# The first filter of a two-layer diffusion trunk, moved from ahead of the first norm to beside it

## The chip, the cores and the metric

The kernel runs on one core of a Trainium2 chip, as one launch. The metric is the device time of that launch in microseconds (us). TensorE does the matmuls, VectorE (DVE) and ScalarE (ACT) the elementwise work and the evacuation of psum, GpSimd (POOL) a few loads, and SyncE (SP) issues nearly all DMA. Each engine works through its own list in order and waits on semaphores for the others.

## The reference, cut to what matters

Two streams, 128 prompt tokens and 1024 sample tokens of width 1024, pass two layers. The sample stream gets a grid position embedding first. Each layer normalises, projects once into four groups of mixers (GLA, a gated linear recurrence with a short convolution, Hyena, HGRN2), joins them, and then runs a gated feed-forward.

```python
xs = x_sample + grid_position_embedding(...)          # 1024 x 1024
mod = silu(c) @ w_mod[l] + b_mod[l]                   # six vectors a layer
u = rmsnorm(x, norm1_g) * (1 + sc1) + sh1
proj = u @ w_in                                       # all mixers' inputs
...
def hyena_filters(L, ...):                            # needs no token at all
    h = sin(sin(pe @ w1 + b1) @ w2 + b2) @ w3
    h = h * exp(-dist * decay_rate)
    return h / sum(abs(h))
full = irfft(rfft(z, n=2L) * rfft(h, n=2L))           # long convolution
```

Four Hyena filters are needed: two layers, each for the sample (L = 1024) and the prompt (L = 128). Each is made in two steps: its taps (h, its weighting by the decay and the sum of its absolute values) and its spectra (sums and differences of halves, then matmuls with transform matrices). None depends on the tokens.

## The kernel before

Tokens lie along the free dimension: 1152 columns, prompt and sample together, cut into three blocks of 384, and the 1024 channels lie in eight tiles of 128 partitions. Two channel tiles of x share a buffer of 128x2304 f32 (1152 KB), so x is four loads; a piece of the modulation weights is 128x2048 f32 (1024 KB). Line 298 is the helper through which all matmuls go, so its rows are told apart by tiles: `pm<-u,ws` are projections (`u` the normalised tokens, `ws` split weights), `pm<-ws,u` the value projections, `ps<-fX,fw` filter taps, `ps<-fH,fM` spectra with the transform matrices `fM`, `ps<-rgx,rgw` the recurrent gates, `pa<-wm,cT` the modulation. One f32 row of a matmul in program order is recorded as two in the trace.

The work that the change touches, in the names of the profile of before:

- `x_in` loads x, adds the position embedding (L1825, VectorE), squares it (L1828 and L1831, ScalarE), sums the squares over the eight channel tiles (L1832, VectorE), sums over partitions on TensorE with ones (`pa`), makes the mean (`hss`, L1841) and an inverse root by some sixteen small VectorE operations (L496 to L508, `rp`).
- `norm_u` transposes and broadcasts that root on TensorE, and makes `ut` (L569) and `u` (L572) on VectorE.
- `taps` of a filter loads its weights and decay into `fX`, and does nine rounds for the sample (five for the prompt): a matmul into `ps`, an exponential `fwn` (L1146, ScalarE), a product `fH` (L1147, VectorE), an absolute value `fab` (L1153, ScalarE), a running sum in `fX` (L1154, VectorE). Then two sums on TensorE (`ones`).
- `spectra` makes sums and differences of the taps (L1189 to L1198), matmuls with `fM`, and stores (L1220, L1222). `fil_mats` (L1232) loads `fM`, four pieces of 576 KB.
- `hgrn_items` are projections whose psum (two buffers, tag m) ScalarE reads twice, into `TT` and `KK` with a sigmoid (L853). `v_proj` evacuates by plain copies (L816). `rg_core` runs the gates: sigmoids (L1032), tanh (L1040), exponential (L1044), square (L1045), square root (L1050) on ScalarE, products and scans on VectorE (L1046 to L1066). Functions that don't share a table cost ScalarE an ACT_TABLE_LOAD between them.

The program is written as generators. `turns` takes a step of each of its generators in rotation. `weave` and `run_norm` run a main generator, and after each step take items from a fill queue (projections) for as many nanoseconds of TensorE as that step declares, so the written order mixes both. A scheduler then orders each engine's list. `filters_b` returns the two generators of one filter, here t0 and s0 for layer 0 of the sample, t1 and s1 for layer 1, tp0, sp0, tp1, sp1 for the prompt.

Of the kernel before, what the change touches and what calls it, by code (L numbers as in the profile page):

```python
# [26 lines left out]
DEPTH = 2  # L27
# [250 lines left out]
class Trunk:  # L278
# [7 lines left out]
    NM = (4, 6)  # L286
# [129 lines left out]
    def mod_load(s, l, c, i):  # L416

        w = s.d("wm")[:, :2048]
        s.nc.sync.dma_start(w.rearrange("p (j n) -> p j n", j=4), s.A["w_mod"][l, c, i])
        if l == 0 and c == s.NM[0] - 1 and i == 1:  # L420
            s.behind = s.nc.cur_bb.bb.instructions[-1]
        return w
# [691 lines left out]
    def taps(s, l, which, box, V):  # L1114
# [8 lines left out]
        X = s.d("fX")  # L1123
        hx = X[:2, 1024:1536]
# [6 lines left out]
        if which == "s":  # L1131
            MV = s.fil_mats()
        else:
            MV = [X[:P, 2048 + 48 * i:2096 + 48 * i].unsqueeze(1) for i in range(5)]
            for i in range(5):
                nc.sync.dma_start(MV[i], s.A["fil_p"][i] if i < 4 else s.A["fin_p"])

# [36 lines left out]
        nc.vector.tensor_tensor(out=ht(0)[:1], in0=ht(0)[:1], in1=sk, op=ALU.add)  # L1174
        V.X, V.ht, V.hx, V.MV = X, ht, hx, MV
        yield

    def spectra(s, l, which, box, V):
# [3 lines left out]
        X, ht, hx, MV = V.X, V.ht, V.hx, V.MV  # L1182
# [620 lines left out]
    def x_in(s, box, V):  # L1803
# [3 lines left out]
        for i in range(4):  # L1807
# [8 lines left out]

        pieces = ((0, 512, s.fw[:, 0:512]), (512, 768, V.H[0][:, 2048:2304]), (768, 1024, V.H[1][:, 2048:2304]),
                  (1024, 1152, s.fw[:, 512:640]))
# [16 lines left out]
        ssq = s.p("a")  # L1835
        for (a, b, ac) in pieces:
            for c in range(a, b, 128):
                i = c // 128
# [6 lines left out]
    def main(s):  # L1845
# [5 lines left out]
        with tc.tile_pool(name="dp", bufs=19) as dp, tc.tile_pool(name="gp", bufs=1) as gp, \  # L1851
# [66 lines left out]
            fb = {w: [] for w in "sp"}  # L1918
# [5 lines left out]
            box = []  # L1924
            (t0, s0, V0), (t1, s1, _) = [s.filters_b(l, "s", fb["s"]) for l in range(DEPTH)]
            (tp0, sp0, _), (tp1, sp1, _) = [s.filters_b(l, "p", fb["p"]) for l in range(DEPTH)]
            ch = itertools.chain
            xi = s.x_in(box, V0)
            na, nb = s.NM
            for _ in s.turns([ch(t0, itertools.islice(s0, nb)), xi, s.mods_pe(0, 0, na, s.AH)]):  # L1930
                pass
            x, xt, y = box

            def rest():
                for _ in s0:
                    yield 2700
            s.fill_add([s.item(rest)], None)
# [4 lines left out]
            def late():  # L1942
                yield from s.mods_pe(0, na, 12, 2)
                s.fill_add([s.v_proj(0, 1, st.u, st.vh)], ("vh", 0))
            s.weave(s.turns([ch(t1, s1, tp0, sp0, tp1, sp1), late()]), s.WB)
# [17 lines left out]
```

## Time and profile before

| | us |
| --- | --- |
| median of 3 runs | 3343.38 (3341.73 to 3345.31) |
| profiled execution, its own time | 3340.47 |
| its span in the trace | 3338.4 |
| first projection matmul starts | 91.24 |
| first gate matmul starts | 272.97 |
| mean granted clock of TensorE | 0.991 of full speed |

The rows further down come from the one profiled execution. A row of a timeline is a run of like instructions on one engine: start, length, engine, line, operation, output and inputs, shape, count, and in brackets how long the engine had stood idle just before and which instruction released it. A row of windows gives the busy time of each engine inside a stretch. The clock column is the granted TensorE clock as a share of 2.4 GHz.

### The profile page before, as it was taken

To read this page: it belongs to the slowest core of one execution; us is meant where nothing else is said; L and a number is where in the kernel's file an instruction comes from. 1 tells how busy PE (TensorE), PEld (TensorE's weight loads), DVE (VectorE), ACT (ScalarE), POOL (GpSimd) and SP (SyncE) were. 2 spreads that over 40 slices of the span, in tenths; PEclk is the share of its full clock that TensorE was granted. 3 is DMA by queue.
4 is the path that set the end of the run, shared out by engine and by line. 5 is a ranking of instruction groups with operands and counts; after the bars stand their busy time and mean duration, and the time that the engine had idled before them with its cause. 6 is when DMAs were issued, how large, how long until landed. Compare 5 with 4: busy or idle time off the path is not lost.

```text
span 3338.4 us, 55402 instructions
## 1 busy us (share of the span) xinstructions
PE 3250.3 (97%) x23886; PEld 3029.7 (91%) x23886; DVE 1742.9 (52%) x3412; ACT 1008.9 (30%) x1774; POOL 27.6 (1%) x101
## 2 busy tenths in 40 slices
PE   7999999999999999999999999999999999999998
PEld 3657878899999999999998888889999999999997
DVE  6635885648463444444457787665653322232326
ACT  5437354333231111111125535432332111111112
POOL 0000000000000000000000000000000000000000
PEclk8999999999999999999999999999999999999999
DMA  7541101224121121222212110113310111111112
GB/s 278 176 158 32 50 17 34 69 103 150 39 80 64 69 91 58 86 73 73 73 58 92 36 45 22 43 60 127 133 51 26 45 45 40 46 36 45 46 45 75
DMA packets 72992, 241.10 MB, mean 72 GB/s; under 512 B 14319, under 2 KB 26469, under 8 KB 60972
## 3 DMA queue, kind: packets, MB, share of 16 engines
q1 hardware_dynamic: 70844, 223.22, 19.2%
q0 software_dynamic: 1904, 14.35, 1.2%
q8 instruction: 187, 3.06, 0.4%
q14 instruction: 57, 0.47, 0.0%
HBM read 207.99 MB, written 29.56 MB: 71 GB/s over the span
## 4 chain that ended last, share of the span: by engine, by line
PE 84%; DVE 9%; ACT 5%; issue 1%; DMA 1%; SPq 0%; DVEq 0%; ACTq 0%
PE pm L298 54%; PE ps L298 26%; PE pa L298 3%; PE pa L301 1%; DVE QQ L686 1%; DVE KK L682 1%; DVE DS L685 1%; DVE ws L342 1%; DVE rgri L1060 0%; ACT ws L341 0%; DMA wr<-w 0%; DVE TT L687 0%; ACT rgri L1032 0%; DVE rgab L1055 0%; ACT rgab L1044 0%
## 5 line engine op out<-in xcount | busy, mean ns | idle before, releaser
L298 PE MATMUL pm<-u,ws 128*128 128x384 f32 x9792 | 1793.0, 340 | 13.5 <-ACT KK L853 4.0
L298 PEld LDWEIGHTS pm<-u,ws 128*128 128x128 f32 x9792 | 1703.1, 188 | 44.6 <-issue 9.5
L298 PE MATMUL ps<-hid,ws 128*128 128x384 f32 x3168 | 559.0, 337 | 0.0
L298 PEld LDWEIGHTS ps<-hid,ws 128*128 128x128 f32 x3168 | 553.7, 188 | 0.6 <-DVE hid L1766 0.2
L341 ACT CAST ws<-wr 128x1024 fp32r<-128x1024 f32 (+3 forms) x234 | 220.3, 941 | 659.5 <-PE ps L298 396.2
L342 DVE TENSOR_TENSOR ws<-wr,ws 128x1024 fp32r<-128x1024 f32 (+3 forms) x234 | 254.6, 1088 | 215.3 <-ACT ws L341 214.3
L1764 DVE TENSOR_TENSOR sg<-sg,pm 128x384 f32<-128x384 f32 x132 | 73.0, 553 | 463.5 <-PE pm L298 463.4
L1508 DVE SCALAR_TENSOR_TENSOR x<-ps,mod,x 128x256 f32<-128x256 f32 (+1 forms) x320 | 158.2, 515 | 275.7 <-PE ps L298 274.4
L1765 ACT CAST hid<-sg 128x384 fp32r<-128x384 f32 x132 | 67.7, 513 | 474.1 <-DVE sg L1764 474.0
L298 PE MATMUL pm<-mh,ws 128*128 128x384 f32 x1152 | 203.8, 337 | 0.7 <-DVE x L1508 0.7
L298 PEld LDWEIGHTS pm<-mh,ws 128*128 128x128 f32 x1152 | 200.9, 188 | 1.6 <-DVE x L1508 1.4
L1758 ACT ACTIVATE sg<-pm 128x384 f32<-128x384 f32 x132 | 64.6, 489 | 225.1 <-PE pm L298 225.1
L470 DVE SCALAR_TENSOR_TENSOR acc<-wm,cT,acc 128x512 f32<-128x512 f32 x168 | 116.1, 745 | 0.2 <-DMA wm<-w_mod 0.2
L298 PEld LDWEIGHTS pm<-ws,u 128*128 128x128 f32 x864 | 107.7, 188 | 8.7 <-issue 3.8
L298 PE MATMUL pm<-ws,u 128*128 128x272 f32 (+1 forms) x864 | 114.9, 289 | 0.6 <-DVE lr L818 0.4
L1766 DVE TENSOR_TENSOR hid<-sg,hid 128x384 fp32r<-128x384 f32 x132 | 73.6, 558 | 58.2 <-ACT hid L1765 58.2
L298 PEld LDWEIGHTS ps<-QQ,DS 64*64 64x64 f32 x3456 | 67.9, 134 | 36.2 <-issue 14.8
L682 DVE TENSOR_TENSOR KK<-KK,TT 128x640 f32<-128x640 f32 x112 | 92.3, 824 | 9.9 <-PE pa L301 6.8
L685 DVE COPY_PREDICATED DS<-masks,ps 128x320 f32<-128x320 uint8 x192 | 89.2, 478 | 14.4 <-PE ps L298 13.7
L298 PE MATMUL ps<-QQ,DS 64*64 64x64 f32 x3456 | 86.0, 230 | 9.3 <-DVE QQ L686 3.5
L686 DVE TENSOR_TENSOR QQ<-QQ,TT 128x640 f32<-128x640 f32 x112 | 91.7, 819 | 2.3 <-PE ps L298 1.8
L541 ACT ACTIVATE sq<-x 128x384 f32<-128x384 f32 x84 | 43.8, 523 | 142.1 <-DVE x L1508 109.0
(307 smaller groups left out, 2623.1 us busy)
## 6 DMA issues: line engine op xcount, KB each, us to landing
wm<-w_mod SPq DMA_DIRECT2D x48, 1024.0 KB, 6.5
wr<-w SPq DMA_DIRECT2D x96, 512.0 KB, 3.3
wr<-w_in SPq DMA_DIRECT2D x48, 512.0 KB, 3.5
dft<-dft_s POOLq DMA_DIRECT2D x12, 1152.0 KB, 5.4
wr<-w SPq DMA_DIRECT2D x32, 320.0 KB, 2.9
xscr<-x SPq DMA_DIRECT2D x8, 1152.0 KB
x<-xscr SPq DMA_DIRECT2D x8, 1152.0 KB, 5.3
wr<-w_out SPq DMA_DIRECT2D x16, 512.0 KB, 3.2
```

The costliest lines, as they stand in the source:

```text
L298: return s.nc.tensor.matmul(out, lhsT, rhs, start=start, stop=stop)
L341: nc.scalar.copy(w[:, 0, :n], raw[:, :n])
L342: nc.vector.tensor_tensor(out=w[:, 1, :n], in0=raw[:, :n], in1=w[:, 0, :n].bitcast(F32), op=ALU.subtract)
L470: nc.vector.scalar_tensor_tensor(out=acc[:, x], in0=wk, scalar=cc, in1=acc[:, x], op0=ALU.mult, op1=ALU.add)
L682: nc.vector.tensor_tensor(out=ka, in0=ka, in1=cap(TT, o + T + h, [[2 * h, n], [-(T + h), 2], [0, h]]), op=ALU.mult)
L685: nc.vector.copy_predicated(Dt[g][:, j], s.masks[:, li].unsqueeze(1).to_broadcast([128, nb, 64]), ps[j])
L686: nc.vector.tensor_tensor(out=qa, in0=qa, in1=cap(TT, o + h, [[2 * h, n], [T - h, 2], [0, h]]), op=ALU.mult)
L1508: nc.vector.scalar_tensor_tensor(out=x[k][:, a:b], in0=ps[:, a - g * GS:b - g * GS], scalar=gcol[:, k, st:st + 1], in1=x[k][:, a:b], op0=A ...
L1758: nc.scalar.activation(out=sg, in_=ps, func=AF.Silu)
L1764: nc.vector.tensor_tensor(out=sg, in0=sg, in1=pp[1], op=ALU.mult)
L1765: nc.scalar.copy(hi[:, 0, sl], sg)
L1766: nc.vector.tensor_tensor(out=hi[:, 1, sl], in0=sg, in1=hi[:, 0, sl].bitcast(F32), op=ALU.subtract)
```

## The change

The first filter's taps and half of its spectra ran in turns with the loading of x, its squares and the first modulation vectors; the rest of its spectra were a fill item beside the first norm. Now x and the modulation vectors come alone; the taps of the first filter are the fill item beside the first norm (behind the recurrent mixer's projections), and its spectra stand at the head of the chain of the other filters, which are woven with the fill queue. The transform matrices are loaded when the first spectra begin. The running sums of squares, which lay in gaps of three tiles in four pieces, get a tile `ssq` and three pieces. The fill queue and all other code stay.

```diff
--- before.py
+++ after.py
@@ -283,7 +283,7 @@
     ORD = ((0, 1, 2), (2, 1, 0))
 
     LG = ((0, 5), (5, 9))
-    NM = (4, 6)
+    NM = 4
     WB = 1800
     AH = 3
     VP, VB = (2, 3, 3), ((1, 2), (0,))
@@ -417,7 +417,7 @@
 
         w = s.d("wm")[:, :2048]
         s.nc.sync.dma_start(w.rearrange("p (j n) -> p j n", j=4), s.A["w_mod"][l, c, i])
-        if l == 0 and c == s.NM[0] - 1 and i == 1:
+        if l == 0 and c == s.NM - 1 and i == 1:
             s.behind = s.nc.cur_bb.bb.instructions[-1]
         return w
 
@@ -1128,9 +1128,8 @@
         sk = X[:1, 1536:2048] if l else s.fh[:1, 1800:2312] if which == "s" else None
         if sk is not None:
             nc.sync.dma_start(sk, s.A["hy_skip"][l])
-        if which == "s":
-            MV = s.fil_mats()
-        else:
+        MV = None
+        if which == "p":
             MV = [X[:P, 2048 + 48 * i:2096 + 48 * i].unsqueeze(1) for i in range(5)]
             for i in range(5):
                 nc.sync.dma_start(MV[i], s.A["fil_p"][i] if i < 4 else s.A["fin_p"])
@@ -1179,7 +1178,7 @@
         nc = s.nc
         h = HC[which]
         Q, P, NT, ncol = h["Q"], h["P"], h["NT"], h["ncol"]
-        X, ht, hx, MV = V.X, V.ht, V.hx, V.MV
+        X, ht, hx, MV = V.X, V.ht, V.hx, V.MV or s.fil_mats()
         if which == "s":
             iP, iM, iRp, iRm = 0, 3, 6, 7
         else:
@@ -1800,7 +1799,7 @@
                 else:
                     yield w
 
-    def x_in(s, box, V):
+    def x_in(s, box):
 
         nc, A = s.nc, s.A
         x, xt = s.xtiles()
@@ -1813,9 +1812,8 @@
         nc.sync.dma_start(pr, A["pos_row"])
         nc.sync.dma_start(pc, A["pos_col"])
         yield
-
-        pieces = ((0, 512, s.fw[:, 0:512]), (512, 768, V.H[0][:, 2048:2304]), (768, 1024, V.H[1][:, 2048:2304]),
-                  (1024, 1152, s.fw[:, 512:640]))
+        sq = s.d("ssq")
+        pieces = [(a, b, sq[:, a:b]) for a, b in ((0, 512), (512, 1024), (1024, 1152))]
         for k in range(KT):
             xs = x[k][:, :L_S].rearrange("p (a b) -> p a b", b=64)
             if k < 4:
@@ -1922,19 +1920,18 @@
             for _ in s.turns([s.filters_a(w, fb[w]) for w in "sp"]):
                 pass
             box = []
-            (t0, s0, V0), (t1, s1, _) = [s.filters_b(l, "s", fb["s"]) for l in range(DEPTH)]
+            (t0, s0, _), (t1, s1, _) = [s.filters_b(l, "s", fb["s"]) for l in range(DEPTH)]
             (tp0, sp0, _), (tp1, sp1, _) = [s.filters_b(l, "p", fb["p"]) for l in range(DEPTH)]
             ch = itertools.chain
-            xi = s.x_in(box, V0)
-            na, nb = s.NM
-            for _ in s.turns([ch(t0, itertools.islice(s0, nb)), xi, s.mods_pe(0, 0, na, s.AH)]):
+            na = s.NM
+            for _ in s.turns([s.x_in(box), s.mods_pe(0, 0, na, s.AH)]):
                 pass
             x, xt, y = box
 
-            def rest():
-                for _ in s0:
+            def taps():
+                for _ in t0:
                     yield 2700
-            s.fill_add([s.item(rest)], None)
+            s.fill_add([s.item(taps)], None)
             st, gen = s.open(0, x, y, None)
             s.run_norm(gen)
             s.x_out(0, xt)
@@ -1942,7 +1939,7 @@
             def late():
                 yield from s.mods_pe(0, na, 12, 2)
                 s.fill_add([s.v_proj(0, 1, st.u, st.vh)], ("vh", 0))
-            s.weave(s.turns([ch(t1, s1, tp0, sp0, tp1, sp1), late()]), s.WB)
+            s.weave(s.turns([ch(t0, s0, t1, s1, tp0, sp0, tp1, sp1), late()]), s.WB)
             s.fill_add(s.hgrn_items(0, st.u, 0, st.hb[0]), ("h0", 0))
             for l in range(DEPTH):
                 st = s.layer(l, st)
```

In rows of the changed program some line numbers are one or two lower than before (L1145 for L1146). Where the norm and the taps now stand on **TensorE**, early in the program: before, the first filter's spectra (`ps<-fH,fM`) stood around the sums of squares (`pa_588`) and the transposes of the root (`ident`, `rp`); the seven taps named `fX_229` had run ahead of these rows.

```order
L298 MATMUL ps_659<-fH_227,fM_233 128x512
L298 MATMUL ps_716<-fH_227,fM_233 128x512
L298 MATMUL pa_656<-sel_9_99,mp_638 128x8
L298 MATMUL ps_728<-fH_228,fM_233 128x512
L298 MATMUL ps_648<-fH_227,fM_233 128x512
L298 MATMUL ps_648<-h_146_644,fex_143 128x512
L298 MATMUL ps_659<-fH_227,fM_233 128x512
L298 MATMUL ps_659<-h_146_644,fex_143 128x512
L298 MATMUL ps_716<-fH_227,fM_233 128x512
L301 MATMUL pa_677<-ident_88,rp_613 18x128
L298 MATMUL ps_716<-h_146_644,fex_143 128x512
L301 MATMUL pa_724<-ident_88,rp_613 18x128
```

After the change, from the root's transposes on, with `fX_561` the first filter's taps and `pm_780` the first projection:

```order
L301 MATMUL pa_650<-ident_88,rp_484 18x128
L298 MATMUL ps_565<-fX_561,fw_147 128x512
L298 MATMUL ps_575<-fX_561,fw_147 128x512
L298 MATMUL ps_594<-fX_561,fw_147 128x512
L298 MATMUL ps_610<-fX_561,fw_147 128x512
L298 LDWEIGHTS seln_82
L298 MATMUL pa_571<-rT_573,seln_82 128x128
L298 LDWEIGHTS seln_82
L298 MATMUL pa_571<-rT_573,seln_82 128x128
L298 LDWEIGHTS seln_82
L298 MATMUL pa_571<-rT_573,seln_82 128x128
L298 MATMUL pm_780<-u_510,ws_772 128x384
```

The spectra are gone from this place, four taps stand between the two broadcasts (`seln`), and the first projection follows with four taps still to come.

The second sample filter on **TensorE** (taps `ps<-fX,fw`; `pa` are modulation, `pm` projections), before:

```order
L298 MATMUL ps_972<-fX_906,fw_147 128x512
L298 MATMUL pm_965<-u_673,ws_957 128x384 x2
L298 MATMUL pm_965<-u_674,ws_957 128x384 x3
L298 MATMUL pm_1017<-u_667,ws_962 128x384 x3
L298 MATMUL pm_1017<-u_668,ws_962 128x384 x3
L298 MATMUL ps_1024<-fX_906,fw_147 128x512
L298 MATMUL pm_1017<-u_669,ws_962 128x384 x3
L298 MATMUL pm_1017<-u_670,ws_962 128x384 x3
L298 MATMUL pm_1017<-u_671,ws_962 128x384 x3
L298 MATMUL pm_1017<-u_672,ws_962 128x384 x3
L298 MATMUL pm_1017<-u_673,ws_962 128x384 x3
L298 MATMUL pm_1017<-u_674,ws_962 128x384 x3
```

and now:

```order
L298 MATMUL ps_1282<-fX_1278,fw_147 128x512
L298 MATMUL ps_1290<-fX_1278,fw_147 128x512
L298 MATMUL pa_1298<-sel_9_99,mp_1288 128x8
L298 MATMUL ps_1301<-fX_1278,fw_147 128x512
L298 MATMUL pa_1309<-wm_1248,cT_107 32x128 x16
L298 MATMUL ps_1328<-fX_1278,fw_147 128x512
L298 MATMUL pa_1309<-wm_1274,cT_107 32x128 x16
L298 MATMUL ps_1354<-fX_1278,fw_147 128x512
L298 MATMUL ps_1364<-fX_1278,fw_147 128x512
L298 MATMUL ps_1375<-fX_1278,fw_147 128x512
L298 MATMUL ps_1402<-fX_1278,fw_147 128x512
L298 MATMUL ps_1428<-fX_1278,fw_147 2x512
```

The projections between its taps have moved ahead of them and ahead of the first gate matmul; 123 matmuls of the HGRN2 projections now stand ahead of that gate matmul where there were 52.

The second prompt filter on **ScalarE**, which has the exponentials `fwn` and absolute values `fab` of its taps, before (`v` are value projections' copies):

```order
L1146 ACTIVATE fwn_1966<-fX_1922,fw_147 48x512
L1150 ACTIVATE fX_1922<-fH_1921 48x512
L816 COPY v_1708<-pm_1937 128x256
L1153 ACTIVATE fab_1969<-fH_1921 48x512
L1146 ACTIVATE fwn_2001<-fX_1922,fw_147 48x512
L816 COPY v_1708<-pm_1972 128x256
L1153 ACTIVATE fab_2004<-fH_1921 48x512
L1146 ACTIVATE fwn_2009<-fX_1922,fw_147 48x512
L341 CAST ws_2126<-wr_2124 128x1024
L1153 ACTIVATE fab_2012<-fH_1921 48x512
L1146 ACTIVATE fwn_2044<-fX_1922,fw_147 2x512
```

and now (`TT` and `KK` are the sigmoids of HGRN2 projections):

```order
L1145 ACT_TABLE_LOAD
L1145 ACTIVATE fwn_2007<-fX_1982,fw_147 48x512
L853 ACT_TABLE_LOAD
L853 ACTIVATE KK_2091<-pm_2099 128x384
L1152 ACTIVATE fab_2010<-fH_1981 48x512
L1145 ACT_TABLE_LOAD
L1145 ACTIVATE fwn_2015<-fX_1982,fw_147 48x512
L853 ACT_TABLE_LOAD
L853 ACTIVATE TT_2092<-pm_2133 128x384
L1152 ACTIVATE fab_2018<-fH_1981 48x512
L1145 ACT_TABLE_LOAD
```

The copies between the exponentials have become sigmoids, with a table load at each alternation; seven of them stand in this filter's rows.

## Rows read from the trace of the kernel before

**Rows 1.** the page's first part: busy time of each engine, share of the span, x instructions.

```profile
PE 3250.3 (97%) x23886; PEld 3029.7 (91%) x23886; DVE 1742.9 (52%) x3412; ACT 1008.9 (30%) x1774; POOL 27.6 (1%) x101
```

**Rows 2.** windows: length, busy us of PE, PEld, DVE, ACT, POOL; clock, DMA share, GB/s.

```profile
0.00:91.24 91.24, 67.30 (x371) 34.60 (x371) 62.83 (x163) 45.78 (x89) 2.31 (x9) 0.83 0.66 256
91.24:272.97 181.73, 179.17 (x1174) 109.91 (x1172) 91.48 (x175) 75.75 (x147) 0.32 (x6) 0.99 0.47 158
272.97:317.60 44.63, 43.59 (x203) 36.63 (x202) 19.84 (x21) 32.97 (x44) 0.00 (x0) 0.95 0.08 26
317.60:3338.40 3020.80, 2960.22 (x22142) 2848.56 (x22142) 1568.71 (x3054) 854.43 (x1495) 24.97 (x86) 1.00 0.18 62
```

**Rows 3.** windows of the first stretch, columns as before.

```profile
40.00:60.00 20.00, 10.20 (x110) 6.53 (x102) 17.75 (x36) 12.44 (x29) 0.00 (x0) 0.59 1.01 423
44.00:48.00 4.00, 0.00 (x0) 0.00 (x0) 4.00 (x6) 2.41 (x5) 0.00 (x0) 0.62 1.01 418
48.00:52.00 4.00, 3.01 (x50) 2.82 (x54) 3.62 (x8) 2.50 (x7) 0.00 (x0) 0.50 1.01 422
60.00:80.00 20.00, 16.61 (x108) 9.63 (x107) 17.28 (x49) 8.52 (x19) 0.00 (x0) 0.84 0.07 27
```

**Rows 4.** timeline of VectorE: start, length, line, output and inputs, wait before.

```profile
51.12 1.22 DVE L1825 TENSOR_TENSOR x<-x,fh 128x1024 f32<-128x1024 f32 x1
...
58.49 0.67 DVE L1832 TENSOR_TENSOR fw<-fw,sq 128x512 f32<-128x512 f32 x1
...
79.94 0.18 DVE L507 TENSOR_TENSOR rp<-rz,one_i 128x18 int32<-128x18 int32 x1
80.16 0.18 DVE L508 TENSOR_TENSOR rp<-rz,rp 128x18 f32<-128x18 f32 x1
86.58 1.67 DVE L569 SCALAR_TENSOR_TENSOR ut<-x,G,pa 128x384 f32<-128x384 f32 x3 [6.24 <-PE pa L298]
```

**Rows 5.** timeline of SyncE, at the filter matrices' loads.

```profile
8.50 2.96 SPq L1232 DMA_DIRECT2D fM<-fil_s  x4
```

**Rows 6.** timeline of TensorE, five places.

```profile
86.39 5.42 PE L298 MATMUL ps<-fH,fM 128*128 128x512 f32 x12
91.24 3.88 PE L298 MATMUL pm<-u,ws 128*128 128x384 f32 x19
...
156.16 1.05 PE L298 MATMUL ps<-ones,fX 128*128 128x2 f32 x8
...
162.88 1.98 PE L298 MATMUL ps<-fH,fM 128*128 128x512 f32 x4 [0.90 <-DVE fH L1190]
...
222.49 8.14 PE L298 MATMUL pm<-ws,u 128*128 128x272 f32 x63
...
285.52 13.55 PE L298 MATMUL pm<-u,ws 128*128 128x384 f32 x75
```

**Rows 7.** timeline of VectorE in the second sample filter's taps.

```profile
121.47 0.69 DVE L1154 TENSOR_TENSOR fX<-fX,fab 128x512 f32<-128x512 f32 x1 [0.70 <-ACT fab L1153]
122.08 0.75 DVE L1147 SCALAR_TENSOR_TENSOR fH<-ps,fw,fwn 128x512 f32<-128x512 f32 x1
123.53 0.69 DVE L1154 TENSOR_TENSOR fX<-fX,fab 128x512 f32<-128x512 f32 x1 [0.70 <-ACT fab L1153]
```

**Rows 8.** timeline of ScalarE, in those taps and in the gate stage.

```profile
122.87 0.63 ACT L1153 ACTIVATE fab<-fH 128x512 f32<-128x512 f32 x1 [0.82 <-DVE fH L1147]
...
300.56 2.23 ACT L1050 ACTIVATE rgab<-rgab 128x1154 f32<-128x1154 f32 x2
302.81 1.28 ACT L853 ACT_TABLE_LOAD   x1
304.11 0.49 ACT L853 ACTIVATE TT<-pm 128x384 f32<-128x384 f32 x1
...
316.65 1.04 ACT L341 CAST ws<-wr 128x1024 fp32r<-128x1024 f32 x1 [1.55 <-DMA wr<-w_in]
317.60 2.47 ACT L1032 ACTIVATE rgri<-ps,vecs 128x385 f32<-128x385 f32 x5
```

## The prediction, made before the changed kernel ran

> **What bounds the kernel now.** I read the page's first part before anything else: TensorE is busy for 97% of the span, VectorE for half, ScalarE for 30% [rows 1]. So time can only come from TensorE's idle stretches, its low clock, or work taken away; the change takes no TensorE work away, it reorders it. Next I cut the span into four stretches, at the first projection matmul, the first gate matmul, and a gate evacuation at 317.60 [rows 2]. From that last row on every engine's list reads the same before and after, apart from tile numbers, so the last 3020.80 us should cost the same and the change is worth what it does to the moment 317.60. Ahead of it TensorE idles 91.24 - 67.30 = 23.9 us in the first stretch, 181.73 - 179.17 = 2.6 in the second and 1.0 in the third. Only the first has much to give, and the later two have much to lose.
>
> In the first stretch VectorE works 17.75 of 20 us from 40 to 60 [rows 3], on the first filter's taps and the first norm's sums alternately. A wide position add still stands at 51.12 and a sum at 58.49, the inverse root ends at 80.16 + 0.18, and the first norm product waits 6.24 us for TensorE until 86.58 [rows 4]; the first projection runs at 91.24 [rows 6]. I call the start of that first norm product T.
>
> **The change, step by step.** *Earlier T.* The four filter-matrix issues stood at 8.50 on SyncE's queue, 2.96 us ahead of the first x load [rows 5]; they go behind, so the x loads start at about 8.5. Four x tiles and five of eight modulation tiles, 4 x 1152 + 5 x 1024 KB = 9.96 MB by their shapes, at the 423 GB/s of [rows 3] take 23.5 us, so the last x tile lands at 32 to 34. In VectorE's new list three sums a round remain (512, 512 and 128 columns, about 1.46 us a round by the 0.67 of [rows 4]). Five rounds stand ahead of the last tile's adds: 34 + 7.3 = 41.5. Two adds of 1.22 and two rounds follow: 47. The TensorE sums and the mean make 49, sixteen small operations at the 0.21 between two rows of [rows 4] make 52.5, transposes and broadcasts make **T = 54** (bounds 46, if sums keep step with the loads, and 59, if ScalarE's squares fall behind).
>
> From T to the first projection it was 4.66 us (86.58 to 91.24). Now sixteen norm operations at 0.55 (1.67 for three, [rows 4]) come before the first weight split, and the second broadcast, which stands ahead of the projection on TensorE, waits for ScalarE's cast (1.04), a table load (1.28) and an exponential [rows 8]: 12.6 us, so the first projection runs at 66.6. **Term: 66.6 - 91.24 = -24.6.**
>
> *Work that moves behind it.* Five of the nine taps, the two column sums and all spectra matmuls of the first filter. A tap is two recorded matmuls, the spectra are 39. Twelve ran in the 4.85 us from 86.39 to 91.24, four in 1.98 [rows 6], 0.40 to 0.50; I take 0.45: 10 x 0.45 + 39 x 0.45 = 22.1, and two sums of 1.0 each (1.05 for one, [rows 6]). **Term: +24.1.** TensorE waits little here. VectorE has behind the first norm block (8.8) a second (8.8), a third in 32 short products (some 11), nine taps of 0.75 + 0.69 = 13 and three weight splits (some 3.7), and waits in eight rounds for ScalarE (0.82 each, 6.6) [rows 7, 8]: 52 to 53 us, so the ninth tap's sum and with it the spectra come at 107, against 39.5 us of projections, taps and modulation that TensorE has queued from 66.6, until 106.1. **Term: +0.9.**
>
> *Second sample filter.* Before, projections stood between its taps on TensorE and the stretch idled 2.6 us in all, 0.90 of it ahead of the spectra [rows 2, 6]. Now the nine taps follow one another. A round passes from exponential to product, absolute value and sum, and takes 123.53 - 121.47 = 2.06 us [rows 7], in which ScalarE stands 0.82 waiting for VectorE [rows 8] and VectorE 0.70 for ScalarE. The loads and first round take 4.7 and the nine rounds 18, 22.7 in all, until the sum can run, and TensorE has 14.6 us queued (taps, modulation, a few value projections): it waits 8.1, and 0.5 before the spectra. **Term: 8.6 - 2.6 = +6.0.** The bounds are +2 (the first rounds run beside the first spectra) and +8.
>
> *The prompt filters.* Before, the first one's butterfly was hidden by 8.14 us of value projections [rows 6]. These now come earlier, so five VectorE operations of 0.67 show: 3.3. In the second, ScalarE's new list alternates the tap exponentials with the sigmoid evacuations TT and KK, with seven table loads between. A load takes 1.28 and the operation behind it starts 1.30 after the load did [rows 8]. From one KK to the next are four loads (5.2) and five operations of 0.5 to 0.6 (2.8), 8 us, and TensorE, whose third projection needs the first pair's bank back, has 4.4 us of matmuls for that time (75 took 13.55, 0.18 each, [rows 6], so 24 take 4.3). It waits about 3.9, twice. **Term: 3.3 + 7.8 = +11.1.** The trace of before has no such alternation of functions, so the bounds are 0 (TensorE holds enough other work) and +16 (each of seven loads shows).
>
> On that price the Trainium skill ("ScalarE: Activation LUTs", section What ACT_TABLE_LOAD costs) differs from the row: it adds a drain of about 1380 ns to each load of 1283 ns. The row agrees on the load and shows no drain, since the next operation starts at once. By the page the seven would cost 7 x 1.38 = 9.7 more, an estimate, and the sum would be +29.4.
>
> *Gate stage.* First gate matmul to 317.60 took 44.6 us [rows 2]. In the new list no projection evacuation delays ScalarE: twelve gates at 0.49 (2.47 for five), eight passes over 1154 columns at 1.12, three loads of 1.28 and one TT make 19.2 until the square roots end; before that end was 302.79 - 272.97 = 29.8 after the first gate matmul [rows 2, 8]. From there to 317.60 it is 14.8 both times (VectorE's scans and the weights of the next projection). That is -10.6; but 71 projection matmuls that stood inside now run before the first gate, 71 x 0.18 = 12.8 [rows 6]. **Term: +2.2** (bounds -3, if the scans too start with less behind them, and +12.8, if ScalarE saves nothing).
>
> *Costed at nothing.* The filter matrices now load when the first spectra begin to be issued, behind the residual copies and weights on SyncE; they are wanted at about 107, and DMA moved 27 GB/s from 60 to 80 [rows 3], so they land in time; uncovered they cost about their 6 us. The new accumulator tile takes a buffer that nothing else wants yet.
>
> **Sum:** -24.6 + 24.1 + 0.9 + 6.0 + 11.1 + 2.2 = **+19.7**. The profiled execution took 3340.47, 2.9 below the median of 3343.38, so 3343.4 + 19.7 = **3363 us**, with a range of its own of 3351 to 3376.
>
> **Rivals.** Changes below 0.2% (6.7 us) count as the same; a measurement of this kernel tells little less.
>
> *Faster: the pace of VectorE and ScalarE does not bind.* If TensorE finds work through the second filter, the prompt filters and the gate stage, what remains is -24.6 + 24.1 + 0.9 - 2.6 + 0 - 1.0 (the idle of [rows 2] goes too) = -3; with the earliest T (46, 8 us sooner) it is -11, some **3332**. For it: ScalarE is busy 30% and VectorE half. Against it: their queues are in order and the loads stand in the list. It decides where T comes 4 us early or more and at most 1 of the waits shows. Chance 0.12.
>
> *The same.* T at 46 to 50 and half of the waits hidden: -6 - 10 on the sum, +4, **3347**. Chance 0.17.
>
> *Slower still: TensorE's clock.* From 44 to 48 TensorE ran no matmul, and from 48 to 52 its granted clock was 0.50, the lower of its two levels (1.2 of 2.4 GHz); over 40 to 60 it was 0.59 with 10.20 us busy, some 4 lost [rows 3]. If the three long lulls that I forecast are followed by 3 us of such loss each, that makes +9, **3372**. For it: those rows; against it: in the second stretch, with its waits of about 1 us, it kept 0.99 [rows 2]. The Trainium skill ("TensorE: Matmul & The Clock Gate", Part 1: The HAM clock gate) states that idleness brings the half rate, and this trace agrees with its 0.50. Chance 0.15.
>
> *The norm does not come earlier,* because x lands late or the squares bind: T at 65 adds 11 to the sum, 3374. Chance 0.04.
>
> That leaves 0.52 for the forecast. Faster 0.12, the same 0.18, slower 0.70. The range of 8 in 10 runs from 3341 to 3378: it leaves out the faster case below and the clock with the page's drains above.
>
> **What would show it.** First projection near 67, first norm product near 54; first spectra after 107; TensorE idle about 8 us among the second filter's taps, with no projection between; two TensorE waits of about 4 us on ScalarE's KK, beside seven table loads; first gate matmul near 303; the gate evacuation of 317.60 near 337; the stretch behind it 3020 to 3022 long. I am wrong if that last stretch changes, if T is not near 54, or if the waits stand elsewhere on engines with time to spare.

## The result, and the profile after

The changed kernel took 3401.27 us (median of 4 runs, 3396.35 to 3404.88) beside 3342.56 for the kernel before: ratio 1.0176, 95% interval 1.0164 to 1.0188, some 59 us slower. The forecast was 3363, with 3378 as the upper end: the direction was right, the size a third of what came. Two details ahead of the prediction were told wrongly: the taps' item stands ahead of the recurrent projections in the fill queue, not behind, and of the seventeen steps of the first filter's spectra six, not half, ran in turns with the loads.

The span of the profiled execution went from 3338.4 to 3400.6. The windows of the kernel after, cut at the same marks as [rows 2] (first projection, first gate matmul, the gate evacuation at which the lists join, the end; columns as there):

```profile
0.00:71.55 71.55, 38.85 (x315) 24.28 (x315) 47.53 (x128) 32.09 (x63) 2.46 (x12) 0.74 0.73 286
71.55:337.14 265.59, 248.77 (x1300) 146.31 (x1299) 109.45 (x203) 98.39 (x176) 0.16 (x3) 0.85 0.36 121
337.14:375.28 38.14, 33.13 (x134) 26.01 (x133) 18.52 (x20) 27.42 (x37) 0.00 (x0) 0.90 0.05 17
375.28:3400.60 3025.32, 2963.59 (x22140) 2852.34 (x22140) 1567.81 (x3054) 853.28 (x1494) 24.77 (x86) 1.00 0.18 62
```

The marks moved from 91.24, 272.97 and 317.60 to 71.55, 337.14 and 375.28. So 57.7 of the 62.2 us arise ahead of the join, as the prediction had it, and 4.5 behind it; the same last stretch took 3020 to 3025 in the profiles of kernels with the change's small parts alone, so the 4.5 tell nothing. Up to the join TensorE does the same matmuls in both kernels: before it was busy for 67.30 + 179.17 + 43.59 = 290.1 us and idle for 27.5, after it is busy for 320.8 and idle for 54.5. **The same matmuls take 30.7 us more, and idleness grows by 27.0.** The clock column says where the first comes from: 0.85 between first projection and first gate, where [rows 2] had 0.99.

The first norm, on VectorE (answering [rows 4]), and TensorE from there (answering [rows 6]):

```profile
54.46 0.18 DVE L508 TENSOR_TENSOR rp<-rz,rp 128x18 f32<-128x18 f32 x1
56.09 1.66 DVE L569 SCALAR_TENSOR_TENSOR ut<-x,G,pa 128x384 f32<-128x384 f32 x3 [1.45 <-PE pa L298]
```

```profile
63.70 0.37 PE L301 MATMUL pa<-ident,rp 128*18 128x128 f32 x1 [7.73 <-DVE ut L569]
64.00 7.19 PE L298 MATMUL ps<-fX,fw 64*128 64x512 f32 x8
71.13 0.50 PE L298 MATMUL pa<-rT,seln 18*128 18x128 bf16 x3
71.55 0.69 PE L298 MATMUL pm<-u,ws 128*128 128x384 f32 x1
72.17 3.78 PE L298 MATMUL ps<-fX,fw 64*128 64x512 f32 x4
75.88 5.25 PE L298 MATMUL pm<-u,ws 128*128 128x384 f32 x22
```

The norm product starts at 56.09 (forecast 54), 30 us earlier than before. But TensorE's third transpose waits 7.73 us for VectorE's norm products, and the second broadcast (`rT`, at 71.13) stands behind eight tap matmuls that take 7.19 us, 0.90 each. After one projection matmul at 71.55 four more tap matmuls stand ahead of the next, so the projections proper begin at 75.88.

The first filter's spectra, then the second sample filter on TensorE, then its taps on VectorE (answering [rows 7]):

```profile
116.00 5.39 PE L298 MATMUL ps<-fH,fM 128*128 128x512 f32 x12 [0.39 <-DVE fH L1189]
...
162.51 1.52 PE L298 MATMUL pm<-ws,u 128*128 128x272 f32 x10
167.49 3.78 PE L298 MATMUL ps<-fX,fw 64*128 64x512 f32 x4 [3.46 <-DMA fX<-hy_w]
...
179.45 8.99 PE L298 MATMUL ps<-fX,fw 64*128 64x512 f32 x10
...
196.92 0.60 PE L298 MATMUL pa<-sel,mp 128*128 128x8 f32 x2 [4.38 <-ACT mp L428]
...
198.01 1.87 PE L298 MATMUL ps<-ones,fX 128*128 128x2 f32 x8
```

```profile
177.77 0.75 DVE L1146 SCALAR_TENSOR_TENSOR fH<-ps,fw,fwn 128x512 f32<-128x512 f32 x1 [1.66 <-PE ps L298]
...
181.62 0.75 DVE L1146 SCALAR_TENSOR_TENSOR fH<-ps,fw,fwn 128x512 f32<-128x512 f32 x1 [1.71 <-PE ps L298]
```

The moved spectra start at 116.00 (forecast 107, TensorE had other work until then) and take 0.45 us a matmul, as priced. In the second filter no projection stands between the taps, as the order showed. TensorE's idle time is 3.46 and 4.38, 7.8 us against the 8.6 of the forecast. But four tap matmuls take 3.78 and ten 8.99. Four of the same taps in the kernel before took half of that:

```profile
126.06 1.98 PE L298 MATMUL ps<-fX,fw 64*128 64x512 f32 x4
```

So VectorE, which was to set a pace of 2.06, now waits 1.66 and 1.71 for TensorE: a round takes 3.85 (177.77 to 181.62). From the end of the last value projection at 164.03 to the sum at 198.01 go 34.0 us, 7.8 of waiting and 26.1 of work; the forecast had 22.7 for the stretch, 8.1 of waiting and 14.6 of work. The windows of this stretch and of the first prompt filter's spectra:

```profile
167.49:205.00 37.51, 33.13 (x228) 17.43 (x228) 16.18 (x31) 12.83 (x23) 0.00 (x0) 0.50 0.33 110
287.27:299.00 11.73, 11.73 (x15) 2.24 (x16) 1.23 (x2) 3.12 (x6) 0.00 (x0) 0.50 0.14 34
```

Both stand at 0.50, the lower of TensorE's two levels, 1.2 GHz. In the second TensorE has no idle time at all. The kernel before has the same fall without any wait, at its own second prompt filter's spectra (48 rows and 48 columns). TensorE had been busy without a gap since 259.17, first with 38 projection matmuls, and two of these matmuls go from 0.95 to 1.94 us (timeline, then windows):

```profile
266.00 1.91 PE L298 MATMUL ps<-fH,fX 48*48 48x512 f32 x4
...
270.52 1.94 PE L298 MATMUL ps<-fH,fX 48*48 48x512 f32 x2
```

```profile
266.00:270.00 4.00, 4.00 (x10) 0.92 (x9) 0.76 (x2) 1.91 (x4) 0.00 (x0) 1.00 0.05 12
270.00:273.00 3.00, 3.00 (x6) 0.53 (x5) 0.00 (x0) 0.58 (x1) 0.00 (x0) 0.54 0.54 118
```

Below, a matmul is called narrow if it uses fewer than 128 rows or fewer than 128 columns of TensorE's array (the figures joined by `*` in a row), and wide if it uses 128 of both.

ScalarE (answering [rows 8]) and TensorE in the prompt filters and the gate stage:

```profile
303.22 1.28 ACT L1145 ACT_TABLE_LOAD   x1
304.51 0.72 ACT L1145 ACTIVATE fwn<-fX,fw 48x512 f32<-48x512 f32 x1
305.25 1.28 ACT L853 ACT_TABLE_LOAD   x1
306.54 0.49 ACT L853 ACTIVATE KK<-pm 128x384 f32<-128x384 f32 x1
306.93 0.62 ACT L1152 ACTIVATE fab<-fH 48x512 f32<-48x512 f32 x1
307.56 1.28 ACT L1145 ACT_TABLE_LOAD   x1
```

```profile
287.27 1.94 PE L298 MATMUL ps<-fH,fX 48*48 48x512 f32 x2 [3.63 <-DVE fH L1196]
...
307.09 6.01 PE L298 MATMUL pm<-u,ws 128*128 128x384 f32 x24 [0.19 <-ACT KK L853]
315.79 1.67 PE L298 MATMUL pm<-u,ws 128*128 128x384 f32 x8 [2.69 <-ACT KK L853]
...
337.14 10.04 PE L298 MATMUL ps<-rgx,rgw 128*128 128x385 f32 x24
...
362.23 10.01 PE L298 MATMUL pm<-u,ws 128*128 128x384 f32 x48 [4.55 <-ACT KK L853]
```

Three of the seven loads are shown; all stand there, each 1.28, each with the next operation 1.29 to 1.30 behind its start, so without the drain that the Trainium skill ("ScalarE: Activation LUTs", What ACT_TABLE_LOAD costs) adds; here the measurement decides. TensorE's waits are 3.63 for the butterfly (forecast 3.3), but 0.19 and 2.69 for KK (forecast 3.9 twice): its own matmuls were slow enough to hide most of the loads, 24 projections taking 6.01 where 4.4 was reckoned. The gate stage, from the first gate matmul to the join, took 38.1 us, where the forecast had 34.0 (44.6 less 10.6): its first matmuls run at the low level, and TensorE waits 4.55 for a KK in it.

### The profile page after: what moved, and what is told of

The parts are those of the page before. It is cut to its first block, busy times and chain, and to the rows that moved or that the text cites. A ratio compares the mean times of both kernels' runs of the same rounds, so it can differ in the third digit from the quotient of the medians.

```text
span 3400.6 us, 55410 instructions
## 1 busy us (share of the span) xinstructions
PE 3284.3 (97%) x23886; PEld 3048.9 (90%) x23886; DVE 1743.3 (51%) x3405; ACT 1011.2 (30%) x1768; POOL 27.4 (1%) x101
## 4 chain that ended last, share of the span: by engine, by line
PE 83%; DVE 9%; ACT 5%; DMA 2%; issue 1%; SPq 0%; DVEq 0%; ACTq 0%
PE pm L298 54%; PE ps L298 25%; PE pa L298 3%; DVE QQ L686 1%; PE pa L301 1%; DVE KK L682 1%; DVE DS L685 1%; DMA x<-xT 1%; DVE ws L342 1%; DMA wr<-w 0%; DVE rgri L1060 0%; DVE TT L687 0%; DVE u L572 0%; DVE ut L569 0%; ACT ws L341 0%
```

## The experiments

Ratios are of each kernel to the kernel before; differences in us are such ratios times 3343, and those of less than some 5 us are not clear of the intervals. The first theory was that lulls bring TensorE's low level and that this level is the missing loss (**clock**); its rival, that the order of the engines' work costs by itself (**pace**).

**The lull among the taps, filled.** In the changed kernel, ahead of the second sample filter's taps:

```diff
+            if l == 1 and which == "s":
+                s.warm(20 if i == 0 else 2)   # matmuls u x u, 128 rows, 384 columns
             ps = s.p("s")
             s.mm(ps[:pp], h2[:, i * P:i * P + pp], w3, start=True, stop=True)
```

> The changed kernel with 38 extra matmuls of 384 columns, whose result is thrown away, issued among the second sample filter's taps (20 ahead of the first, 2 ahead of each later one); they are extra work and change no output. Theory clock: the loss there is TensorE at its low level (0.50 from 167.5 to 205, 29 us busy) after a lull of 3.46 us, so filling the lull with 6.5 us of work at 0.17 each makes the stretch shorter: the total falls by 8 to 14 us, and the granted clock of the taps is near 1. Theory pace: the loss is the round of VectorE and ScalarE and the loads, and the extra work is at best hidden: 0 to +7 us, whatever the clock.

Ratio 1.0175 (1.0157 to 1.0192): nothing gained, nothing lost, as the pace theory had it and the clock theory had not. The extra matmuls were all put ahead of the taps, 22 of them into the lull, which they filled from 163.91 on (the first tap runs at 168.58). Behind them the first four tap matmuls took 1.98, the high level; then the level fell all the same (windows of this run, columns as above):

```profile
160.00:180.00 20.00, 18.57 (x141) 11.11 (x140) 5.03 (x8) 6.45 (x11) 0.00 (x0) 0.84 0.69 246
180.00:200.00 20.00, 17.20 (x102) 9.80 (x104) 7.38 (x15) 5.91 (x11) 0.00 (x0) 0.59 0.30 106
```

So the lull is not what brings the low level here, as the clock theory had it; and the 4.1 us of extra work in it cost nothing, since they took its place.

**Extra matmuls between the rounds.** On the same stretch, each pair made to wait for its round:

```diff
+            if l == 1 and which == "s" and i < nt:
+                pw = s.p("m")
+                for j in range(2):
+                    s.mm(pw, s.ident, ht(i), start=(j == 0), stop=(j == 1))
             yield
```

> The changed kernel with two extra f32 matmuls of 512 columns behind each of the second sample filter's eight tap rounds, on the round's own result, so that they can only stand between the rounds; some 14 us of extra work at the high level, whose result is thrown away. Theory clock: a thinly filled TensorE is granted the low level there, and the slow matmuls are what holds the rounds up; filled, it keeps the high level, and the stretch from the first tap to the sum (167.5 to 198.0, 30.5 us) becomes 24 to 28: total -3 to -8 us. Rival (the rounds themselves take the time, the level only shows it): the extra work adds to it, +10 to +25 us.

Ratio 1.0187 (1.0173 to 1.0201), 3.7 us above the changed kernel, not clear of it: between both expectations. The windows of this run:

```profile
170.00:175.00 5.00, 5.00 (x7) 1.82 (x6) 2.19 (x3) 3.00 (x6) 0.00 (x0) 0.50 0.10 43
175.00:180.00 5.00, 5.00 (x37) 2.38 (x37) 0.92 (x2) 0.58 (x2) 0.00 (x0) 0.96 0.00 0
180.00:185.00 5.00, 5.00 (x41) 2.28 (x40) 2.05 (x3) 1.91 (x4) 0.00 (x0) 1.00 0.44 129
...
195.00:200.00 5.00, 5.00 (x56) 2.17 (x48) 1.44 (x2) 1.24 (x2) 0.00 (x0) 1.00 0.63 210
```

The level is 1.00 from 180 on, where it was 0.50. The 32 extra matmuls are busy for 17.0 us (the sum of their rows), and the stretch from the first tap to the sum grew from 30.5 to 35.0. So 12.5 us of 17.0 were given back, by the taps and modulation pieces that run twice as fast and in the wait of 4.38, which is gone. The low level is a cause of the loss in this stretch, and wide matmuls between the taps lift it.

**The same question in the prompt filters.** First with matmuls on 48 rows in the butterfly's wait:

```diff
             nc.scalar.copy(ht(ib), tmp)
+            if which == "p":
+                pw = s.p("a")
+                for j in range(2):
+                    s.mm(pw, s.ident[:P], ht(ia), start=(j == 0), stop=(j == 1))
```

> The changed kernel with four extra f32 matmuls of 512 columns (on 48 rows) in each prompt filter, behind its butterfly, whose result is thrown away: some 3.4 us of extra work at the high level, put into the wait of 3.63 us ahead of the first spectra at 287.27, behind which the granted clock is 0.50 to 299 and 0.66 to 326. Theory clock: the wait is what brings the low level there, so with it filled the matmuls from 287 to 299 (11.7 us busy at 0.50) run in 6 to 7: the first gate matmul comes 4 to 10 us earlier than 337.1. Rival (thinly filled engines bring it, not the wait): the gate comes 0 to 4 us later.

Ratio 1.0183 (1.0169 to 1.0197); the first gate matmul came at 344.04, 6.9 later, more than either side had expected; 17 projections had also changed sides of the second butterfly. The wait is filled, and the level behind it is as low as before. The filler is itself narrow, so this shows only that narrow work does not hold the level:

```profile
284.00:288.00 4.00, 3.67 (x8) 1.56 (x8) 3.91 (x8) 1.78 (x3) 0.00 (x0) 0.87 0.00 0
288.00:300.00 12.00, 12.00 (x16) 2.16 (x15) 0.47 (x1) 2.49 (x5) 0.00 (x0) 0.50 0.13 33
```

Then with wide matmuls, held in place by one narrow one each:

```diff
+    def wide(s, src, P, n):
+        pw = s.p("a")[:, :384]
+        s.mm(pw, s.ident[:P], src[:P, :384], start=True, stop=False)
+        for i in range(n):
+            w = s.wu[i % 8]
+            s.mm(pw, w[:, 0, :128], w[:, 0, :384], start=False, stop=(i == n - 1))
...
+            if which == "p":
+                s.wide(ev, P, 5)              # behind each output; behind each butterfly on ht(ia)
```

> The changed kernel with seven groups of extra matmuls in each prompt filter, behind its butterflies and its outputs: one f32 matmul on 48 rows that holds the place, and five matmuls on 128 rows and 384 columns behind it, some 1.5 us a group at the high level, 21 us in all, whose result is thrown away. Theory (TensorE is granted the low level where only narrow matmuls run, and the high one with wide ones between): the granted clock from 287 to 340 is above 0.9 where it was 0.50 to 0.76, the slow matmuls give back some 15 us, and the first gate matmul, at 337.1 in the changed kernel, comes at 336 to 346. Rival (the level follows the waits on the other engines): the clock stays near 0.6 and the extra work adds in full, the gate comes at 360 or later.

```profile
284.00:290.00 6.00, 6.00 (x20) 2.63 (x19) 3.63 (x7) 1.62 (x4) 0.00 (x0) 1.00 0.00 0
290.00:300.00 10.00, 10.00 (x33) 4.60 (x32) 0.00 (x0) 1.91 (x4) 0.00 (x0) 1.00 0.18 39
300.00:310.00 10.00, 10.00 (x18) 3.74 (x17) 1.49 (x2) 4.72 (x8) 0.00 (x0) 0.50 0.22 62
310.00:320.00 10.00, 10.00 (x31) 6.28 (x30) 3.54 (x5) 9.87 (x12) 0.00 (x0) 0.65 0.00 0
320.00:330.00 10.00, 10.00 (x57) 8.77 (x56) 5.83 (x12) 5.45 (x9) 0.00 (x0) 1.00 0.16 54
330.00:340.00 10.00, 10.00 (x35) 4.86 (x34) 4.57 (x8) 4.02 (x8) 0.00 (x0) 1.00 0.11 26
```

The level is 1.00 with them, drops to 0.50 from 300 to 310, where the second prompt filter's taps stand with one group only among them, and is back at 1.00 from 320 on, behind a run of projections; so the level above 0.9 that was expected throughout is missed from 300 to 320. The first gate matmul comes at 348.25, 2 us above the range, after 13 groups of 1.91 each from start to start at the high level, 24.8 us of work, for 11.1 us more: some 13.7 are given back, near the 15 expected. As a kernel it is slower: ratio 1.025 (1.0231 to 1.0269). The profiled execution, 3416.83, is the shortest of its four (median 3425.15); what the others gave back is not shown.

**The table loads, taken away** (other gates are computed: the exponential of a thousandth of the input):

```diff
-                    nc.scalar.activation(out=dst, in_=ps, func=AF.Sigmoid, scale=sgn)
+                    nc.scalar.activation(out=dst, in_=ps, func=AF.Sigmoid if l or un else AF.Exp,
+                                         scale=sgn if l or un else 0.001 * sgn)
```

> The changed kernel with the first layer's first HGRN2 gate evacuations TT and KK taken through the exponential (of a thousandth of the input) in place of the sigmoid, so the seven table loads of the second prompt filter are gone; it computes other gates. Theory pace (as predicted): the table loads make two waits, which go: -6 to -10 us. Theory clock: the projections there run at the low level after an earlier lull of 3.63 us and cover the loads, only the 2.9 us of waits seen go: -2 to -4 us, and the clock stays at 0.5 from 287.

Ratio 1.0156 (1.0137 to 1.0174), 6.7 us below the changed kernel, though the intervals overlap; the first gate matmul comes 7.8 earlier, at 329.39. This is the pace theory's number: the alternation costs about what the prediction put on it (7.8), though only 2.9 of it is to be seen as waits of TensorE. The rest is busy time: from 287.3 to the first gate matmul TensorE is busy for 41.8 us in place of 47.0, at 1.00 from 310 on, where the changed kernel had 0.77 to 326.

**The projections held back** behind the prompt filters, by two tiny matmuls each that take a psum buffer of theirs:

```diff
+            if which == "p":
+                pw = s.p("m")
+                s.mm(pw[:, :64], s.ident[:P], ht(ia)[:, :64], start=True, stop=True)
```

> The changed kernel with two tiny matmuls of 64 columns in each prompt filter that take a buffer of the projections' psum, so that the scheduler leaves the HGRN2 projections behind the prompt filters, as it stood before the change; the table loads between sigmoids and exponentials go, and 71 or more projections are back in the gate stage. Theory of a fixed stock of cover: what the gate stage gets back the prompt filters lose: total within 5 us of the changed kernel. Rival (the alternation and the projections run ahead are a loss of their own, as predicted, 11.1 + 2.2): 8 to 14 us less.

Ratio 1.0202 (1.0188 to 1.0216), 8.7 us above the changed kernel: both expectations fail. The gate stage got its cover back and the loads went, but the prompt filters, up to 319 without wide matmuls, idle and run at the low level:

```profile
280.00:300.00 20.00, 14.97 (x22) 3.42 (x23) 7.95 (x16) 4.84 (x9) 0.00 (x0) 0.50 0.08 20
300.00:320.00 20.00, 13.28 (x26) 4.61 (x25) 11.88 (x22) 7.71 (x13) 0.00 (x0) 0.50 0.11 31
```

**The change in parts.** Five kernels tell its parts apart: from the changed kernel, the taps put back in turns with the loads, the spectra left in the chain, and the spectra put into the taps' item beside the norm; from the kernel before, the own tile alone, with the late matrices, and with all spectra beside the norm.

```diff
-            for _ in s.turns([s.x_in(box), s.mods_pe(0, 0, na, s.AH)]):
+            for _ in s.turns([t0, s.x_in(box), s.mods_pe(0, 0, na, s.AH)]):
```

> Half of the change undone: the first filter's taps run in turns with the loading of x as before, its spectra stay at the head of the woven chain. Theory clock and order: the later stretches lack projections as in the changed kernel, so the low clock among the second filter's taps stays; the first projection moves back to 80 to 88; total within 8 us of the changed kernel. Rival (the taps beside the norm do the harm): 20 us or more below the changed kernel.

```diff
-                for _ in t0:
+                for _ in ch(t0, s0):
                     yield 2700
```

> The changed kernel with the first filter's spectra behind its taps in the same fill item beside the norm, so that the recurrent projections come later and stand again between the second filter's taps. Theory clock and order: no lull there, no low clock, so the 30 us of slow matmuls go and the earlier norm may show: 3335 to 3355. Rival (the early norm and its order cost by themselves): 3375 to 3400.

```diff
-        pieces = ((0, 512, s.fw[:, 0:512]), (512, 768, V.H[0][:, 2048:2304]), ...
+        sq = s.d("ssq")
+        pieces = [(a, b, sq[:, a:b]) for a, b in ((0, 512), (512, 1024), (1024, 1152))]
```

> The kernel before with one part of the change alone: the running sums of squares get their own tile and three pieces in place of four. By the rows 7 sums of 0.42 and 9 squares go, on a VectorE that is busy 17.75 of 20 us there: 0 to -4 us against before. The theory that the loss lies in the order of the filters expects no loss here; a loss of more than 2 us would put part of it on this tile.

```diff
-        if which == "s":
-            MV = s.fil_mats()
...
+        X, ht, hx, MV = V.X, V.ht, V.hx, V.MV or s.fil_mats()
```

> The kernel before with two parts of the change: own tile for the sums, and the transform matrices loaded when the first spectra begin. Taps and spectra stand as before. Theory order: x lands 5.6 us earlier, the norm is a little earlier, -2 to -8 us against before. Rival (late matrices make the spectra wait): 0 to +8 us.

```diff
-    NM = (4, 6)
+    NM = (4, 0)
```

> The kernel before with own tile and late matrices, and with none of the first filter's spectra ahead of the norm: its taps stay in turns with the loading of x, all its spectra are the fill item beside the norm. So the norm comes earlier, as the change wants, but the taps stay ahead and the second filter keeps its projections. Theory cover: the first projection moves to 78 to 84, the later stretches keep the high level, 3 to 15 us below before. Rival (any spectra moved behind the norm cost what they gain, or the low level comes there too): within 4 us of before or above it.

| kernel | taps of filter 1 | its spectra | ratio | interval | us |
| --- | --- | --- | --- | --- | --- |
| own tile only | with loads | 6 steps with loads, rest beside norm | 0.9998 | 0.9989 to 1.0007 | -0.7 |
| own tile, late matrices | with loads | the same | 0.9981 | 0.9972 to 0.9990 | -6.4 |
| the same | with loads | beside norm | 1.0017 | 1.0008 to 1.0026 | +5.7 |
| the same (half undone) | with loads | head of chain | 1.0123 | 1.0107 to 1.0138 | +41.1 |
| the same | beside norm | beside norm | 1.0097 | 1.0082 to 1.0112 | +32.4 |
| the change | beside norm | head of chain | 1.0176 | 1.0164 to 1.0188 | +58.8 |

Late matrices gain 5.7 on top of the tile, in the range expected. Moving the spectra from beside the norm to the chain costs 35.4 with the taps ahead and 26.4 with them beside the norm; moving the taps costs 26.7 with the spectra beside the norm and 17.7 with them in the chain. For the half undone both expectations are missed (within 8 us of the change, or 20 and more below): it lies 17.7 below, with its first projection at 76.17 for 80 to 88, so both halves carry the loss. With the taps left ahead and the spectra beside the norm the theory had 3 to 15 us below before; it came out 5.7 above, as its rival had it, though the first projection runs at 74.81. With the spectra beside the norm the second filter has its projections back, and its windows, the taps in them too, read

```profile
140.00:185.00 45.00, 43.16 (x345) 29.47 (x345) 21.70 (x30) 16.20 (x32) 0.00 (x0) 1.00 0.47 160
```

while the whole is still 32.4 us slow: its 3375.4 lie above the 3335 to 3355 expected and just inside the rival's 3375 to 3400 (the early norm and its order cost by themselves). The lulls have moved to other places, one of 9.54 us at 97.74 ahead of the first filter's sum. The profiles split each loss, up to the evacuation at which the lists join:

| taps of filter 1 | its spectra | TensorE busy | idle |
| --- | --- | --- | --- |
| before | | 290.1 | 27.5 |
| with loads (late matrices) | 6 steps with loads | 287.6 | 26.1 |
| with loads | beside norm | 288.0 | 38.7 |
| beside norm | beside norm | 300.4 | 48.4 |
| with loads | head of chain | 316.3 | 46.2 |
| beside norm (the change) | head of chain | 320.8 | 54.5 |

Moving the spectra into the chain slows TensorE's matmuls most; and each kernel that has less work ahead of the norm is idler: of the change's loss ahead of the join about half, 27.0 of 57.7 us, is idleness.

**How much ahead of the norm.** From the kernel with tile and late matrices, nine and twelve in place of six steps of spectra in turns with the loads (`NM = (4, 9)`, `NM = (4, 12)`):

> The kernel before with own tile and late matrices, as in the seventh run, and nine in place of six steps of the first filter's spectra in turns with the loads, that is less work moved beside or behind the norm. Theory: each piece moved ahead fills the time in which x lands, until the norm itself is late: -2 to +3 us against the seventh run. Rival (the optimum is later): +4 or more.

> The same with twelve steps. Theory: past the point where TensorE's queue ahead of the norm is as long as the loads, the norm's transposes wait behind spectra: 0 to +6 us against the seventh run.

0.9993 (0.9984 to 1.0002) and 0.9995 (0.9986 to 1.0004): 4.0 and 4.7 us above the kernel with six (nine were expected within -2 to +3, the rival had +4 or more; twelve within 0 to +6). Of 0, 6, 9 and 12 steps six is the best, against nine and twelve by no more than the intervals allow. That kernel, the change's two small parts without its large one, is faster than the kernel before: 3336.87 beside 3343.58. Its first norm product starts at 79.59 in place of 86.58, its first two windows read

```profile
0.00:84.26 84.26, 62.25 (x370) 32.66 (x371) 61.28 (x154) 42.98 (x79) 2.30 (x9) 0.88 0.70 274
84.26:268.60 184.34, 181.78 (x1175) 110.48 (x1173) 92.75 (x177) 77.32 (x149) 0.32 (x6) 0.98 0.47 157
```

and against [rows 2] idleness ahead of the first projection falls from 23.9 to 22.0 us and busy time from 67.3 to 62.3, with nothing moved behind.

## Why the prediction was right in direction and wrong in size

- **The join, and the order of events: right.** The loss arises ahead of the common tail; norm, missing projections, loads and waits stand where the order had put them. The tail of 3020 to 3022 came out at 3025.
- **Earlier T: nearly right.** The norm product came at 56.09 for 54 and the first projection 15.5 behind it for 12.6, so the term was -19.7 for -24.6. The second part is 2.9 long because the second broadcast stands behind eight taps at 0.90.
- **Waits: right in sum, in part by luck.** From the first projection to the join idleness grew by (16.8 + 5.0) - (2.6 + 1.0) = 18.2; the terms for waits gave 0.9 + 6.0 + 11.1 = 18.0. But the prompt filters' waits were 6.5 for 11.1, and 4.0 of the 18.2 lie in the gate stage, where the sum had none. The other 8.8 of the 27.0 lie ahead of the first projection (32.7 us idle for 23.9).
- **The step that failed is the one that gave the matmuls that stay where they were, in the second filter and the prompt filters, the time they had taken before.** The sum has terms for moved work and for waits and none for the level of what remains; the clock stood only as a rival, +9 with a chance of 0.15. From the first projection to the first gate matmul the forecast was 54.9 us more (24.1 + 0.9 + 6.0 + 11.1 + 12.8), and 83.9 came: idleness grew by 14.3 for 18.0, busy time by 69.6 for 36.9. The moved spectra were priced rightly (0.45). By an estimate from the windows, in which work at 0.50 would take half the time at 1.00, 16.6 of the 33.13 busy us of the second filter were lost, and 11.3 of the 22.54 from 287.27 to 310.00.
- **What it had wrong in the mechanism.** The prediction tied the low level to lulls, with 3 us of loss behind each of three. The runs showed in its place that a lull filled with wide work changes nothing in the total (1.0175), that narrow matmuls alone fall to 0.50 without any lull (270 to 273 in the kernel before), and that wide ones among them bring 1.00, in the taps and in the prompt filters. The loss therefore lasts as long as the narrow stretch: 33 us busy in the second filter, not 3. The kernel before showed it already: the 0.95 of its third window in [rows 2] begins behind those prompt spectra, with no wait ahead.
- **Which cover was lost** is the other side of it. The projections that stood among the taps, and the value projections among the prompt filters, were counted for the waits that they hide. They also held the level. The change uses them up beside the norm and among the second filter's spectra.
- **Table loads:** 7.8 forecast, 6.7 measured (not clear of noise by itself), but mostly as busy time and only in part as waits.
- **Costed at nothing:** the late matrices gain 5.7 by themselves, which stood in the sum as part of T; the own tile is free.

Not shown is why the taps' move and the spectra's move do not simply add (17.7 or 26.7, 35.4 or 26.4), what each lull of the early norm costs by itself, and whether the rows or the columns of the array, or both, set the level.

## What to carry to other kernels

Work that needs no input belongs into the time in which the input loads, even if the input's own first step is later for it, up to a point (six steps of the spectra here, while nine and twelve gained nothing): TensorE has nothing else there, and behind it each such piece took cover from another stretch. Wide matmuls are cover in two ways, for the waits of a narrow chain and for the clock under it, so count for each stretch what stands between its narrow matmuls before moving it. Price not only the matmuls that move but those that stay, at the level that their stretch will then be granted. A part of a change that does well alone (here the loads' order) is worth trying without the rest.

## What was not expected of the hardware

- TensorE was granted 0.50 while the records show it busy without a gap (11.73 us of 11.73 from 287.27). Stretches recorded as equally busy stand at either level: 10.00 of 10.00 us at 1.00 with wide matmuls among the narrow, from 290 to 300 in the run with wide groups, and at 0.50 nearly without, from 300 to 310. The Trainium skill ("TensorE: Matmul & The Clock Gate", Part 1: The HAM clock gate) has the level follow how busy the engine has been; in these rows the records' busy time does not tell it, and the width of the matmuls does.
- The granted clock of a trace's first 40 us is not to be trusted here. The clock column shows 0.95 from 20 to 40 in the kernel before, yet 64 modulation matmuls took 3.42 us at 31.68 there; they took 3.64 at 188.89 in the changed kernel at 0.50, and 1.95 at 152.38 before at 1.00. The durations say that the kernel starts at the low level, with the narrow taps and modulation pieces alone.
